# Reordering ScalarE and VectorE work around the norms of a hybrid decoder block: squares, weight splits and form splits put behind other instructions

## The chip, the core and the metric

The kernel runs on one core of one Trainium2 chip. A core has five engines with instruction queues of their own: TensorE (PE: matmuls, with weight loads PEld shown apart), VectorE (DVE), ScalarE (ACT), GpSimd (POOL) and SyncE (SP, which here only issues DMAs). Each queue is worked through in order; engines wait for each other by semaphores. The metric is the device time of one launch in microseconds (us), the median of several runs.

## What is computed

One residual block on 512 tokens of 1024 channels, all float32:

```
z = rms_norm(x) @ w_in                            # pool, rnn, rnn gate and two branch gates
y_pool = pool_mixer(u_pool) @ w_pool_out          # trailing means over 2, 4, 8, 16 tokens
y_rnn  = rg_lru_branch(u_rx, u_rg) @ w_rg_out     # conv, gated linear recurrence, GeLU gate
x2 = x + rms_norm((gate_pool * y_pool + gate_rnn * y_rnn) @ w_o)
up = rms_norm(x2) @ w_up                          # 2 x 3072 columns
hid = gelu(causal_dwconv(up[:, :3072])) * up[:, 3072:]
x3 = x2 + rms_norm(hid @ w_down)
out = x3 + sigmoid(rms_norm(x3) @ w_ple_gate) * rms_norm(p @ w_ple_proj)
```

`rms_norm` divides a token's row by its root mean square and multiplies by a gain. `p` is the per-layer input embedding (256 wide).

## The kernel before

**Three matmuls for one.** TensorE multiplies operands rounded to a shorter form of float32. Each operand is therefore kept as two parts, a *high* part (`hi`, a rounding copy made on ACT) and a *low* part (`lo`, source minus high part, a subtraction on DVE); `split` (line 193) makes both. `mm3` (line 220) issues high x high (line 222), high x low (line 223) and low x high (line 224). So each weight block costs one ACT copy and one DVE subtraction, and a matmul can start when the high parts are there but stops at the second or third step if a low part is late.

**Seven products for eight.** The large products (`w_rg_out`, `w_o`, `w_up`, `w_down`) are cut into two by two blocks and computed with seven block products of sums of blocks. The sums of the activations are called *forms* and numbered 1 to 7: 1, 2 and 4 are blocks themselves, 5, 6, 7 and 3 are differences and sums (`rg_form` for the recurrent branch, `form` and `form_split` for the up product). Sums of weight blocks come partly from DRAM, where DMAs of the POOL queue add them up. The first pair of up blocks (`p == 0`) is computed plainly, with the blocks `PLAIN = (11, 21, 12, 22)` and half the tokens at a time.

**Stages.** TensorE's order is written out by hand. What matters here, with the times of the profile before:
- to 225 us: input product, pool mixer and recurrent branch, ending with the pool branch's output product: eight weights `("wpo", m)`, each of twelve 512-wide matmuls. Beside it the forms of the recurrent branch are made: with weight m goes form `LATE_FORMS[m]`, that is 5, 6, 3, 7, 2 for m = 0 to 4. `weight(key)` prepares four keys ahead (`AHEAD`).
- 225 to 300 us: the seven products with `w_rg_out`, then those with `w_o`.
- 285 to 330 us: the norm and the residual add for four token tiles of 128 tokens. `x2_sum(t)` squares the two halves of a tile on ACT (line 501, sum accumulated and read), adds the sums on DVE (line 512), takes the power -1/2 on POOL (line 496), and multiplies and adds on DVE (lines 999 and 1004). `x2_out(t)` stores the tile, squares it again, and writes the normed tile `h2n` (line 1078). `h2_tile(t)` transposes it on PE (line 1015), splits both halves (line 1034), and copies two blocks of each half in float32 to `h2f` (line 1042), from which the forms are made. The tiles take turns with the embedding's product (`ple_tile(t)`, evacuated by one DVE copy, line 846, and one ACT copy, line 847) and the first up products: blocks 11 and 21, transposes of tile 2, blocks 12 and 22, transposes of tile 3, product (1,1), then the four plain blocks for the other half of the tokens (`O_AFTER`, line 48). `ple_norm(t)` computes the embedding's norms: two squares, sum, power, and a copy to `rp` (line 855).
- 330 to 355 us: first gated tiles. `gated_half` makes the convolution (one ACT and two DVE instructions, lines 1153 and 1155) and the GeLU; the bank is then given back by an ACT copy (line 1201) so that product (1,6) can go on in it. `hidden` (line 1171) multiplies with the other half, after which `up_product` can write its bank (line 1145). Meanwhile the forms 5, 6, 7, 3 are made (line 1207) and split.
- 355 to 545 us: the loop over pairs of up blocks, seven products each; then the down product, the last norms, and the embedding's gate.

**Who sets the order.** On ACT, DVE, POOL and SP a planner orders the instructions: it simulates the program with its own costs and takes, whenever an engine is free, the ready instruction that stands first in the program, where `urgent()` and `high_priority` move instructions forward. `behind(ins, name)` (line 154) is an edge that makes the planner place `ins` after the named instruction of the same engine; it adds no semaphore. `last_copy`, `last_sub` and `last_low` name the newest high copy and low subtraction. A buffer of a pool (`raw`: 6, `t`: 5, `m`: 25, `C` and `A`: 4 each) that is still in use makes its next user wait; two engines never read one PSUM bank at once, the later in the program waits.

**Names in the profile.** `ps` is a PSUM bank, `m` a slot of the `mid` pool, `t` a temporary, `C` and `A` the large tiles that hold activations in two parts, `h` hidden tiles, `raw` a weight as loaded, `s` one column of sums, `rb` the discarded output of a square.

Of the kernel before, what the change touches and what calls it, by code (L numbers as in the profile page):

```python
# [83 lines left out]
def block_kernel(  # L84
# [272 lines left out]

    ready, low_of = {}, {}
    nxt = [0]
# [27 lines left out]
    def up_form(p, f):  # L387
# [21 lines left out]
        else:  # L409
            t = b[p, {2: 21, 3: 22, 5: 0}[f]]  # L410
        if p == 0 and f in PLAIN[2:]:
            late.append((f, t))
            return
        hi, lo = (v.rearrange("p (j c) -> p j c", j=2) for v in parts_of(D))
        split(hi, lo, t)
        if (p, f) == (0, PLAIN[1]):
            behind(last_sub[0], h2n_done[1])
        if p == 1 and f != 1:
# [5 lines left out]
        if p > 1 and f == 3:  # L424
            behind(last_copy[0], z6_done[p])
        ready["up", p, f] = (hi, lo)

    def late_splits():
# [8 lines left out]
    def prep(key):  # L437
# [24 lines left out]
        if key == order[0]:  # L462
            for a, b in FIRST:
                ACT.copy(hi[:, a:b], raw[:, a:b])
                sub(lo[:, a:b], raw[:, a:b], hi[:, a:b].bitcast(F32))
        else:
            ins = ACT.copy(hi, raw)  # L467
            if key[0] == "wpg" and key[2] == 1:
                behind(ins, last_copy[0].ins.name)
            with tc.high_priority(offset=2 * URGENT if key[0] == "wpg" and key[2] == 0 else 300 if key[0] == "in" and key[1] >= 12 else 0):  # L470
                ins = sub(lo, raw, hi.bitcast(F32))
                low_of[key] = ins.ins.name
            if key[0] == "wpg" and key[2] == 1:
                behind(ins, last_low[0])
# [13 lines left out]

    last_pow, last_square = [None], [None]

# [19 lines left out]
    def rstd_from(sums):  # L510
        v = tiny()
        V.scalar_tensor_tensor(v, sums[0], EPS, sums[1], ALU.add, ALU.add)  # L512
        return rsqrt(v)
# [318 lines left out]
    rp = {}  # L832
    h2n_done, h2f_done, z_copied, hid_done, summed = {}, [None], [None], [None], {}
    z6_done, o_done, ple_done, late = {}, {}, {}, []

# [91 lines left out]
    for m in range(KD):  # L927
        w = weight(("wpo", m))
        if m in LATE_FORMS:
            rg_form(LATE_FORMS[m])  # L930
        pas.append(bank())
        for k in range(4):
# [136 lines left out]

    def x2_out(t, after=None):  # L1070
        res = [xr[t, 0], xr[t, 1]]
        for h in range(2):
            nc.sync.dma_start(x2d[t * P : (t + 1) * P, h * S : (h + 1) * S], res[h])
        with urgent():
            r = rstd_of(res, after=after)
            for h in range(2):
                h2n[t, h] = slot()
                ins = V.scalar_tensor_tensor(h2n[t, h], res[h], r, g_pre[h], ALU.mult, ALU.mult)
                h2n_done[t] = ins.ins.name

# [69 lines left out]
    def gated_half(j, pg):  # L1150
        a = temp()
        with urgent():
            ACT.activation(a, pg, AF.Identity, scale=c1(C_FW + 2 * NJ + j), bias=c1(C_FB + j))
            for d in (1, 2):
                V.scalar_tensor_tensor(
                    a[:, d:], pg[:, : S - d], c1(C_FW + (2 - d) * NJ + j), a[:, d:], ALU.mult, ALU.add
                )
        act(a, a, AF.Gelu_apprx_tanh)
        act_g[j] = a
# [14 lines left out]
    for t in range(NT):  # L1174
# [3 lines left out]
        if t == 1:  # L1178
            h2_tile(1)
            late_splits()  # L1180
            x2_out(2, h2_done[0])
            x2_sum(3, (oz[1], o5[:, 1]))
        if t == 2:
            x2_out(3, ple_done[0])
    for t in range(NT):
        ple_norm(t, ple_outs[t], ple_done[0])
    for kind, n in O_AFTER:
        if kind == "tr":
            h2_tile(n)
        elif kind == "up":  # L1190
            up_plain(n, 0)
# [12 lines left out]
    def form(f, a, b, op=ALU.subtract):  # L1204
        for k in (0, 2):
            d[f, k] = slot()
            V.tensor_tensor(d[f, k], a[k], b[k], op)
# [7 lines left out]
    with urgent():  # L1215
        form(5, h2f[21], h2f[22])
        form(6, {k: d[5, k] for k in (0, 2)}, h2f[11])
        form_split(6)
    form_split(5, True)
    form(7, h2f[11], h2f[21])  # L1220
    form_split(7, True)
    form(3, {k: d[6, k] for k in (0, 2)}, h2f[12], ALU.add)
    form_split(3, True)

# [15 lines left out]
    for i in range(2):  # L1240
        hidden(i, ub[i], None)
    down_sums = sums_of("wd")
    for p in range(1, NPAIR + 1):
# [265 lines left out]
```

## Time and profile before

| what | value |
|---|---|
| median of 3 runs | 705.51 us (705.23 to 705.91) |
| profiled execution | 706.08 us, span 704.1 us |
| TensorE busy | 693.9 us, 99% of the span |
| weight loads busy | 638.9 us, 91% |
| VectorE, ScalarE, GpSimd busy | 592.0, 454.1, 95.9 us |
| DMA traffic | 175.71 MB, mean 250 GB/s |
| granted TensorE clock | 1.000 |

The span runs from the first to the last instruction; the launch around it makes up the rest of the profiled execution's time. A row of the timeline has the start and length in us, engine, line of the kernel, operation, output <- inputs by tile name, shapes, and how many like instructions were merged (x2); in brackets stands how long the engine had been idle and what ended that. A CAST is an ACT copy to the short format. L191 is the subtraction of every split, L195 and L467 are its copies, L501 every square of a norm.

### The profile page before, as it was taken

The numbers are of one execution on the slowest core, as the hardware profiler recorded it, in microseconds if no ns is written. First come the engines' busy times: TensorE is split into PE (matmuls) and PEld (weight loads), VectorE is DVE, ScalarE is ACT, GpSimd is POOL, SyncE is SP. The second block draws the span as 40 slices with busy tenths as digits, with TensorE's granted clock in tenths as the row PEclk, the third lists the DMA queues.
The fourth block names the chain that finished last, engine by engine and source line by source line (L and its number), as shares of the span: only waits on it lengthen the run. The fifth ranks groups of instructions, "written<-read, shape, count | busy, mean of one in ns | idle before, by whom it ended". The sixth has DMA issues, their size and how long they took to land.

```text
span 704.1 us, 11599 instructions
## 1 busy us (share of the span) xinstructions
PE 693.9 (99%) x4423; PEld 638.9 (91%) x4423; DVE 592.0 (84%) x772; ACT 454.1 (64%) x693; POOL 95.9 (14%) x123
## 2 busy tenths in 40 slices
PE   9999999999999999998999999999999999999997
PEld 8888888888888998898999999999999888888886
DVE  5698645999749898886999999999999988989972
ACT  5857789934447575478866677666667747666631
POOL 0311231322000000111011211111111210001100
PEclk9999999999999999999999999999999999999999
DMA  8998999999888997864496896897699799968111
GB/s 314 411 305 257 258 244 222 277 259 283 254 316 298 315 366 251 323 216 142 131 322 210 201 249 232 196 249 243 170 223 369 253 300 332 332 213 276 49 61 61
DMA packets 67287, 175.71 MB, mean 250 GB/s; under 512 B 6048, under 2 KB 6688, under 8 KB 66848
## 3 DMA queue, kind: packets, MB, share of 16 engines
q1 hardware_dynamic: 49808, 124.64, 49.4%
q0 software_dynamic: 17280, 50.34, 31.0%
q8 instruction: 35, 0.57, 0.3%
q14 instruction: 20, 0.16, 0.1%
q10 hardware_dynamic: 144, 0.00, 0.0%
HBM read 162.37 MB, written 62.91 MB: 320 GB/s over the span
## 4 chain that ended last, share of the span: by engine, by line
PE 73%; DVE 13%; ACT 6%; DMA 3%; issue 3%; POOL 1%; SPq 0%; DVEq 0%; ACTq 0%
PE ps L222 23%; PE ps L224 23%; PE ps L223 23%; DVE lo L191 3%; PE ps L575 3%; ACT m L166 2%; DVE m L713 1%; DMA parts<-hi 1%; ACT t L166 1%; ACT hi L195 1%; POOL s L496 1%; DVE m L640 1%; DVE t L784 1%; ACT rb L501 1%; PE ps L684 1%
## 5 line engine op out<-in xcount | busy, mean ns | idle before, releaser
L191 DVE TENSOR_TENSOR lo<-raw,hi 128x1024 fp32r<-128x1024 f32 (+2 forms) x199 | 230.4, 1184 | 48.3 <-ACT hi L467 29.3
L222 PE MATMUL ps<-A,hi 128*128 128x256 f32 (+1 forms) x672 | 212.3, 316 | 1.2 <-ACT ps L1145 0.7
L224 PE MATMUL ps<-A,lo 128*128 128x256 f32 (+1 forms) x672 | 211.6, 315 | 0.0
L223 PE MATMUL ps<-A,hi 128*128 128x256 f32 (+1 forms) x672 | 211.6, 315 | 0.0
L467 ACT CAST hi<-raw 128x1024 fp32r<-128x1024 f32 (+1 forms) x118 | 118.2, 1012 | 59.3 <-PE ps L224 19.8
L222 PEld LDWEIGHTS ps<-A,hi 128*128 128x128 f32 x672 | 128.4, 191 | 9.6 <-issue 1.0
L224 PEld LDWEIGHTS ps<-A,lo 128*128 128x128 f32 x672 | 128.4, 191 | 6.8
L223 PEld LDWEIGHTS ps<-A,hi 128*128 128x128 f32 x672 | 128.4, 191 | 6.6
L222 PE MATMUL ps<-C,hi 128*128 128x256 f32 x376 | 103.9, 276 | 1.8 <-ACT C L195 1.1
L223 PE MATMUL ps<-C,hi 128*128 128x256 f32 x376 | 103.4, 275 | 0.3 <-DVE C L191 0.3
L224 PE MATMUL ps<-C,lo 128*128 128x256 f32 x376 | 103.3, 275 | 0.0
L195 ACT CAST hi<-raw 128x1024 fp32r<-128x1024 f32 x78 | 80.6, 1052 | 23.2 <-PE ps L223 13.7
L222 PE MATMUL ps<-hi,A 128*128 128x512 f32 x224 | 85.2, 380 | 0.0
L224 PE MATMUL ps<-hi,A 128*128 128x512 f32 x224 | 85.0, 379 | 0.0
L223 PE MATMUL ps<-lo,A 128*128 128x512 f32 x224 | 85.0, 379 | 0.0
L222 PEld LDWEIGHTS ps<-C,hi 128*128 128x128 f32 x376 | 71.9, 191 | 2.7 <-ACT C L195 1.2
L223 PEld LDWEIGHTS ps<-C,hi 128*128 128x128 f32 x376 | 71.9, 191 | 0.6 <-DVE C L191 0.5
L224 PEld LDWEIGHTS ps<-C,lo 128*128 128x128 f32 x376 | 71.9, 191 | 0.0
L307 POOL DMA_DIRECT2D wdsum<-in_w_down_dram x36 | 33.1, 1056 | 150.0 <-ACT t L1143 63.8
L496 POOL TENSOR_TENSOR s<-s,mhalf 128x1 f32<-128x1 f32 (+1 forms) x21 | 16.1, 769 | 260.6 <-DVE s L512 238.6
L224 PEld LDWEIGHTS ps<-hi,A 128*128 128x128 f32 x224 | 42.4, 189 | 6.0
L223 PEld LDWEIGHTS ps<-lo,A 128*128 128x128 f32 x224 | 42.4, 189 | 5.8
(202 smaller groups left out, 1068.7 us busy)
## 6 DMA issues: line engine op xcount, KB each, us to landing
raw<-in_w_up_dram SPq DMA_DIRECT2D x46, 512.0 KB, 5.7
wdsum<-in_w_down_dram POOLq DMA_DIRECT2D x36, 512.0 KB, 7.6
raw<-in_w_in_dram SPq DMA_DIRECT2D x32, 512.0 KB, 8.8
raw<-wdsum SPq DMA_DIRECT2D x24, 512.0 KB, 8.5
raw<-in_w_down_dram SPq DMA_DIRECT2D x18, 512.0 KB, 7.0
wosum<-in_w_o_dram POOLq DMA_DIRECT2D x12, 512.0 KB, 9.2
wdsum<-wdsum POOLq DMA_DIRECT2D x12, 512.0 KB, 6.3
raw<-wosum SPq DMA_DIRECT2D x8, 512.0 KB, 6.2
```

The lines of the kernel that those rows point to most:

```text
L166: ins = ACT.activation(o, i, func, **kw)
L191: return V.tensor_tensor(o, a, b, ALU.subtract)
L195: last_copy[0] = ACT.copy(hi, src)
L222: PE.matmul(o, ah, bh, start=start, stop=False, **kw)
L223: PE.matmul(o, ah, bl, start=False, stop=False, **kw)
L224: PE.matmul(o, al, bh, start=False, stop=stop, **kw)
L307: ins = nc.gpsimd.dma_start(o, i, **kw)
L467: ins = ACT.copy(hi, raw)
L496: last_pow[0] = nc.gpsimd.tensor_tensor(y, v, mhalf[:, :n], ALU.pow).ins.name
L501: ins = ACT.activation(rb, v, AF.Square, scale=1.0 / 32.0, accum_out=s)
L575: PE.matmul(rx[m], a[:, o : o + P], turns(b), start=k == 0 and i == 0, stop=k == KD - 1 and i == 2)
L640: return V.tensor_tensor(row(o), back(ps), row(rb), ALU.mult)
```

## The change

No instruction is added or removed; the order on ACT and DVE and the place in the program change, in five parts:
1. *Branch forms behind pool weights.* The copy and subtraction of the branch form made with weight m are put behind those of weight m + 4 (at most 7).
2. *Three up weights late.* Of the plain blocks, 21 now joins 12 and 22 in `late`: split in `late_splits`, its copy behind token tile 1's last copy (line 1042), its subtraction behind that of tile 1. Before, its split came with its load, the subtraction behind normed tile 1.
3. *Fourth norm's sum first.* `x2_sum(3)` comes ahead of `x2_out(2)` in the program, and normed tile 2 goes behind the fourth tile's sum of squares.
4. *Embedding squares behind token tiles' copies.* `ple_norm` of embedding tiles 0 and 1 goes behind tile 2's copies, of 2 and 3 behind tile 3's copies; before, all four stood behind the last embedding tile's copy.
5. *Third up form behind gated tiles.* The subtractions of weights (1,5) and (1,7) leave the place beside their copies: that of (1,5) goes behind the convolution of the second gated tile, that of (1,7) behind `hidden`. Form 3's split goes behind `hidden` too, and its two float32 blocks are taken from the pool `t` instead of `m`.

```diff
-        if p == 0 and f in PLAIN[2:]:
+        if p == 0 and f != PLAIN[0]:
             late.append((f, t))
             return
         hi, lo = (v.rearrange("p (j c) -> p j c", j=2) for v in parts_of(D))
+        if (p, f) in ((1, 5), (1, 7)):
+            ins = ACT.copy(hi, t)
+            behind(ins, h2_done[0])
+            later[f] = hi, lo, t
+            ready["up", p, f] = (hi, lo)
+            return
         split(hi, lo, t)
-        if (p, f) == (0, PLAIN[1]):
-            behind(last_sub[0], h2n_done[1])
...
+    def later_low(f):
+        hi, lo, t = later[f]
+        last_sub[0] = sub(lo, t, hi.bitcast(F32))
+        last_low[0] = last_sub[0].ins.name
...
             ins = ACT.copy(hi, raw)
+            last = ins.ins.name
...
                 low_of[key] = ins.ins.name
+                copy_of[key] = last
...
     def rstd_from(sums):
         v = tiny()
-        V.scalar_tensor_tensor(v, sums[0], EPS, sums[1], ALU.add, ALU.add)
+        last_stat[0] = V.scalar_tensor_tensor(v, sums[0], EPS, sums[1], ALU.add, ALU.add).ins.name
         return rsqrt(v)
...
         if m in LATE_FORMS:
             rg_form(LATE_FORMS[m])
+            behind(last_copy[0], copy_of["wpo", min(m + AHEAD, KD - 1)])
+            behind(last_sub[0], low_of["wpo", min(m + AHEAD, KD - 1)])
...
-    def x2_out(t, after=None):
+    def x2_out(t, after=None, stat=None):
...
                 ins = V.scalar_tensor_tensor(h2n[t, h], res[h], r, g_pre[h], ALU.mult, ALU.mult)
-                h2n_done[t] = ins.ins.name
+                if stat is not None:
+                    behind(ins, stat)
...
             for d in (1, 2):
-                V.scalar_tensor_tensor(
+                ins = V.scalar_tensor_tensor(
                     a[:, d:], pg[:, : S - d], c1(C_FW + (2 - d) * NJ + j), a[:, d:], ALU.mult, ALU.add
                 )
+        conv_done[0] = ins.ins.name
...
             h2_tile(1)
             late_splits()
-            x2_out(2, h2_done[0])
             x2_sum(3, (oz[1], o5[:, 1]))
+            x2_out(2, h2_done[0], last_stat[0])
         if t == 2:
             x2_out(3, ple_done[0])
-    for t in range(NT):
-        ple_norm(t, ple_outs[t], ple_done[0])
     for kind, n in O_AFTER:
         if kind == "tr":
             h2_tile(n)
+            for t in (n - 2) * 2, (n - 2) * 2 + 1:
+                ple_norm(t, ple_outs[t], h2f_done[0])
...
-            d[f, k] = slot()
+            d[f, k] = temp() if f == 3 else slot()
...
     form_split(5, True)
+    later_low(5)
+    behind(last_sub[0], conv_done[0])
     form(7, h2f[11], h2f[21])
     form_split(7, True)
     form(3, {k: d[6, k] for k in (0, 2)}, h2f[12], ALU.add)
-    form_split(3, True)
...
     for i in range(2):
         hidden(i, ub[i], None)
+    later_low(7)
+    behind(last_sub[0], hid_done[0])
+    form_split(3, True)
+    behind(last_sub[0], hid_done[0])
```

More of the change, by code (lines that the diff above doesn't have):

```diff
@@ L356, in block_kernel @@
             plan(("wpg", kp, h), rows2(w_ple_gate, kp, h))
-    ready, low_of = {}, {}
+    ready, low_of, copy_of = {}, {}, {}
     nxt = [0]
@@ L487, in pick @@
         return t[0][:, a:b], t[1][:, a:b]
-    last_pow, last_square = [None], [None]
+    last_pow, last_square, last_stat = [None], [None], [None]
     rb = const.tile([P, S], F32, tag="rb", name="rb")
@@ L832, in block_kernel @@
     rp = {}
-    h2n_done, h2f_done, z_copied, hid_done, summed = {}, [None], [None], [None], {}
-    z6_done, o_done, ple_done, late = {}, {}, {}, []
+    h2f_done, z_copied, hid_done, summed = [None], [None], [None], {}
+    z6_done, o_done, ple_done, late, later, conv_done = {}, {}, {}, [], {}, [None]
     def ple_tile(t):
```

## The prediction

> **What bounds the kernel now.** I read the page first, then busy time by stretches of 10 us, then the waits of TensorE, then the timeline at each place where TensorE stood still. A difference under 0.2%, some 1.4 us, is about what a measurement of this kernel can't tell from none.
>
> ```profile
> span 704.1 us, 11599 instructions
> PE 693.9 (99%) x4423; PEld 638.9 (91%) x4423; DVE 592.0 (84%) x772; ACT 454.1 (64%) x693; POOL 95.9 (14%) x123
> ```
>
> TensorE (PE) is the bound: its order is fixed by hand, and a time saved counts only if PE had been waiting. The stretches, columns PE, weight load (PEld), DVE, ACT and POOL busy, clock, DMA share and GB/s, show where it did:
>
> ```profile
> 200.00:210.00 10.00, 10.00 (x48) 8.79 (x47) 3.88 (x5) 4.61 (x7) 0.00 (x0) 1.00 0.84 329
> 210.00:220.00 10.00, 9.36 (x44) 7.90 (x43) 9.74 (x13) 7.33 (x10) 0.00 (x0) 1.00 0.98 344
> 320.00:330.00 10.00, 7.89 (x64) 7.08 (x63) 5.25 (x14) 7.48 (x24) 2.08 (x4) 1.00 0.41 151
> 340.00:350.00 10.00, 8.77 (x76) 8.39 (x75) 9.39 (x15) 9.85 (x17) 0.00 (x0) 1.00 0.30 95
> 390.00:400.00 10.00, 10.00 (x92) 10.00 (x91) 10.00 (x13) 8.05 (x13) 3.12 (x3) 1.00 0.70 177
> 400.00:410.00 10.00, 10.00 (x92) 10.00 (x91) 8.84 (x9) 5.65 (x11) 1.03 (x1) 1.00 1.10 223
> ```
>
> Between the first load and the tail PE idles in three stretches alone: 0.64, 2.11 and 1.23 us. The clock is 1.00 throughout, so no time hides there. The waits of PE name them (us in all, times, longest); the sum of these six rows, 4.0, is the idle of the three stretches:
>
> ```profile
> PE ps L222 <- ACT C L195: 1.1, 1, 1.1
> PE ps L222 <- ACT ps L1145: 0.7, 1, 0.7
> PE ps L222 <- ACT m L1042: 0.7, 2, 0.6
> PE ps L224 <- DVE lo L191: 0.6, 1, 0.6
> PE ps L222 <- ACT ps L1201: 0.5, 1, 0.5
> PE ps L223 <- DVE C L191: 0.3, 1, 0.3
> ```
>
> Idle understates what a wait costs, because matmuls overlap. Two waits by the starts:
>
> ```profile
> 213.36 0.38 PE L223 MATMUL ps<-m,hi 128*128 128x512 f32 x1
> 214.38 0.48 PE L224 MATMUL ps<-m,lo 128*128 128x512 f32 x1 [0.64 <-DVE lo L191]
> 214.70 0.38 PE L222 MATMUL ps<-m,hi 128*128 128x512 f32 x1
> ...
> 348.24 0.28 PE L224 MATMUL ps<-A,lo 128*128 128x256 f32 x1
> 349.26 0.38 PE L222 MATMUL ps<-A,hi 128*128 128x256 f32 x1 [0.75 <-ACT ps L1145]
> ```
>
> Undisturbed, 512-wide matmuls start 0.21 apart (48 in the 10 us from 200) and 256-wide ones 0.11 (92 in the 10 us from 390). The first wait makes steps of 1.02 and 0.32 out of two of 0.21: it costs 0.92, the last 0.11 of it in a slow first step. The second makes 1.02 out of 0.11, 0.91, and 1.02 with such a step behind it. So a wait costs its idle time plus about 0.27. Seven waits (the third row has two) of 3.98 us idle cost 3.98 + 7 x 0.27 = 5.9 us: 0.9 at the first place (A), 2.11 + 4 x 0.27 = 3.2 at the second (B), 1.23 + 2 x 0.27 = 1.8 at the third (C). That is all that can be had.
>
> By the idle time of matmuls alone it would be 3.98. The Trainium skill (Perfetto Trace Analysis, Identifying the Most-Contended Engine) calls matmul busy time a poor measure, since pipelined instructions look smaller, and would have the weight loads' busy time read instead; by that, each stretch against a full one of its kind, (8.79 - 7.90) + (10.00 - 7.08) + (10.00 - 8.39) = 5.4 us are open. The steps between starts side with the page.
>
> **Place A, branch forms behind pool weights.** Queues of ACT and DVE at the wait:
>
> ```profile
> 209.69 2.00 ACT L195 CAST A<-C 128x1024 fp32r<-128x1024 f32 x2
> 211.59 0.61 ACT L467 CAST hi<-raw 128x512 fp32r<-128x512 f32 x1
> 213.63 0.62 ACT L467 CAST hi<-raw 128x512 fp32r<-128x512 f32 x1 [1.43 <-DMA raw<-in_w_pool_out_dram]
> ...
> 210.76 2.36 DVE L191 TENSOR_TENSOR A<-C,A 128x1024 fp32r<-128x1024 f32 x2 [0.26 <-ACT A L195]
> 213.64 1.33 DVE L191 TENSOR_TENSOR lo<-raw,hi 128x512 fp32r<-128x512 f32 x2
> ```
>
> PE waits for the low part of the fifth pool-out weight, which runs at 213.64 behind the low parts of branch forms 5 and 6 (2.36), as its high part ran behind their copies (2.00). The change adds no instruction; it puts each form behind the weight four ahead. Without the forms in front the copy can run near 209.7 and the low part end by 211; PE wants it at 213.58. Next late is the sixth weight: its load ends at 213.6, its two parts by about 215.0, and PE wants the low part at 213.58 + 12 x 0.215 = 216.2, so 1.1 us are left. The forms are first used when this product ends, ten us on; they wait in the same queues, and the loads behind them stay in their order on SP. Gain 0.9; bounds 0 and 0.9, and I take the whole, the cover being 1.1.
>
> **Place B, the last token tiles.** These rows hold the chain:
>
> ```profile
> 313.06 0.61 ACT L847 COPY m<-ps 128x512 f32<-128x512 f32 x1
> 313.85 1.46 POOL L496 TENSOR_TENSOR s<-s,mhalf 128x1 f32<-128x1 f32 x1 [2.80 <-DVE s L512]
> 319.17 0.54 POOL L496 TENSOR_TENSOR s<-s,mhalf 128x1 f32<-128x1 f32 x1 [3.87 <-DVE s L512]
> 319.75 1.41 DVE L1078 SCALAR_TENSOR_TENSOR m<-m,s,m 128x512 f32<-128x512 f32 x2 [0.66 <-POOL s L496]
> 321.68 1.28 DVE L191 TENSOR_TENSOR C<-ps,C 128x512 fp32r<-128x512 f32 x2
> 322.12 1.04 PE L1015 MATMUL ps<-ident,m 128*128 128x128 f32 x8
> 322.40 0.37 ACT L1042 COPY m<-ps 128x256 f32<-128x256 f32 x1 [2.67 <-DVE C L191]
> 327.51 1.05 ACT L195 CAST C<-ps 128x512 fp32r<-128x512 f32 x2
> ```
>
> and, as one row for the squares (L501) in a stretch, with ACT's busy time:
>
> ```profile
> 318.90:329.30 10.40, 5.84 (x16) 1.00 0.51 168
> ```
>
> PE stands at 323 and 325 for the copies of token tile 2 (L1042), and at 327 and 328 for the high and low parts of tile 3, whose transposes ended at 323.15 (322.12 + 1.04). Tile 2's copies waited for its low parts (321.68), those for the normed tile 3 (319.75), that for the fourth norm's sum, whose power ran only at 313.85. Between the copies, and ahead of tile 3's casts, stand the eight squares of the embedding's norms with their accumulator reads, 5.84 in all, 0.73 each.
>
> Fourth sum first: its inputs come out of the product that ends ahead of the embedding tiles, so its two squares (1.5), sum, power and two adds can follow the third sum's at once, some ten us earlier, on POOL too ahead of the third tile's power. The normed tile 3 then hangs on the copy of embedding tile 2 (L847, 313.06) alone: 313.7, two squares 1.5, power 0.54, 1.41, and the 0.7 of hand-overs give 317.9 instead of 321.2. Low parts of tile 2 then end at 319.2, its copies by 320, when PE wants them at 323.0: both L1042 waits go, with 3 us to spare. The other side: tile 1's casts are pushed back by up to 1.5 on ACT, against the 1.1 that the third edit frees in front of its low parts.
>
> Squares behind the copies: four (2.9 us) now run between tile 2's copies and tile 3's casts, 320 to 323, four behind tile 3's copies. Tile 3's casts start at about 323.2, low parts end by 325.6; PE wants them from 323.0 + 24 x 0.11 = 325.6 on, half 0 first, whose low part ends at 324.9. Both waits go. The embedding tiles hold their slots no longer than 3 us more, while slots come free from the residual tiles.
>
> Up weights late: the copy and low part (1.2) of block 21 move from in front of tile 1's low parts to behind tile 1's copies, ahead of 12 and 22. Tile 1's low parts so start 1.1 earlier. I put tile 1's copies at 310, the high part of 21 at 311, its low part at 312.1 to 313.3 (the latter if DVE first runs the normed tile 2, 1.4). PE reaches block 21 72 matmuls of 0.11 and eight transposes (0.9) ahead of 322.12, at 313.2, and wants its low part at 313.4. This is the tightest spot. Its raw buffer is freed 4 us later, so the load of block (1,5), then pled and x2d stores behind it on SP, start later; their users come 20 us on.
>
> Bounds for B: 3.2, and 3.2 less a stall at block 21 of up to 1.4 + 0.92 + 0.27 = 2.6. The 0.92 is the power's 1.46 against 0.54: it is slow here when a low part runs beside it. On this the Trainium skill (GPSIMD Engine Reference, Specifications) says that POOL shares its SBUF interfaces with VectorE and contends with VectorE instructions of two SBUF inputs, which a low part has; by it three late low parts near these powers speak against the change, and the rival below takes it up. I take 2.8: full gain less one scrap of 0.4, the size of the smallest wait there is (the third row of PE's waits has 0.7 in two, the longest 0.6, which leaves some 0.15 idle, plus 0.27), nearer to the estimate of the copies than to the far bound.
>
> **Place C, into the first transformed products.** First the low parts (L191) among the conv's steps as one row with DVE's busy time, then the two queues:
>
> ```profile
> 336.20:340.40 4.20, 2.42 (x2) 1.00 0.72 219
> ```
>
> ```profile
> 340.31 0.74 DVE L1155 SCALAR_TENSOR_TENSOR t<-ps,col,t 128x510 f32<-128x510 f32 x1
> 347.07 0.69 DVE L191 TENSOR_TENSOR A<-m,A 128x512 fp32r<-128x512 f32 x1 [0.61 <-ACT A L195]
> 347.68 1.28 DVE L1171 TENSOR_TENSOR h<-t,ps 128x512 f32<-128x512 f32 x2
> 348.88 6.90 DVE L191 TENSOR_TENSOR lo<-raw,hi 128x1024 fp32r<-128x1024 f32 x6
> ...
> 338.69 0.36 ACT L1201 COPY ps<-ps 128x256 f32<-128x256 f32 x1 [2.11 <-DVE t L1155]
> 348.84 0.63 ACT L1145 ACTIVATE ps<-ps 128x256 f32<-128x256 f32 x2
> ```
>
> The first wait is for L1201, which needs the last conv step (340.31), behind two low parts, (1,5) and (1,7), 2.42 together. Moved behind the conv, they bring it 2.4 forward; the wait was 0.5. The second is for L1145, which needs the gated tiles (347.68), behind form 3's low parts (2 x 0.6) and 0.61 of waiting for their copy. With form 3 and the low part of (1,7) behind, 1.2 + 1.2 + 0.6 = 3.0 fall out ahead of L1171. But PE arrives 2.8 earlier by place B. DVE starts this stretch with tile 3's low parts, which also end earlier, 325.6 against 329.4, or 3.8; two of the four embedding norms, each with a wait of DVE for POOL of 0.66 as at 319.75, add 1.3. So the gated tiles end near 349.0 - 3.8 - 3.0 + 1.3 = 343.5 and the (1,7) product is due at 349.26 - 1.8 - 2.8 = 344.7 (place A shifts all alike). L1145 needs 0.4 of that; the moved low part of (1,7) runs until 344.7 and is wanted at 344.9. Form 3's temporaries take the last two of the five temp buffers, which are free then; its product comes 8 us later. The cost lies between 0 and today's wait with its restart, 1.0 once more; one scrap, 0.4, is near the middle. C gains 1.8 - 0.4 = 1.4.
>
> **Sum.** 0.9 + 2.8 + 1.4 = 5.1 us. The profiled execution took 706.08 (its span and 1.98 around it), so 701.0 by its own time; it lies 0.57 above the median of 705.51, and the median so comes to 700.4. The loop behind keeps PE full with DVE at 8.84 and 10.00 of 10, so it passes the gain on, and the tail is untouched.
>
> **Rivals.**
> 1. *Block 21 is late* (or tile 1's copies ahead of it). For: three us of room shrink to 0.1 to 1.3; a slow power adds 0.92. Against: ACT and DVE lose 1.5 us of squares and a low part in front. PE waits up to 2.6 and the gain is 5.9 - 2.6 - 0.4 = 2.9: 702.6.
> 2. *ACT and DVE stay the bound at C.* The chain of waits runs through ACT, DVE and POOL from 300 to 349; ACT is at 9.85 of 10 there. If the four squares (2.9) land ahead of the conv and forms, C's waits come back, doubled: 5.9 - 3.6 = 2.3: 703.2. Against it: ACT idled 2.11 ahead of L1201.
> 3. *The moves do nothing*: the planner had ordered so by its own costs and shifts its fillers into the new holes; each wait is replaced by one like it: 705.5. Against it: each new order is an edge that it has to keep.
> 4. *Slower.* The loop's order shifts: 3.6 us of low parts (1,7), form 3, (1,4) are pushed to where six already stand in a row (348.88, 6.90), and the six raw buffers turn later. If in each of the ten turns PE then waits for one low part behind an add, 1.2 us, the whole is 12 - 5.9 = 6.1 slower: 711.6. It decides from (5.9 + 1.4)/10 = 0.73 a turn. Against it: the loop's code is the same, it shows no idle PE, and a delay that comes once is paid once.
>
> **How the numbers follow.** Forecast with scraps from none to twice those taken, 699.6 to 701.2: 0.58. Rival 1: 0.14. Rival 2: 0.13. Rival 3: 0.05. Rival 4: 0.10. The range from 699.5 (nothing waits, less the spread of the runs) to 704.0 holds the first three, 0.85. Faster 0.85, same 0.05, slower 0.10.
>
> **What would show it.** Right: PE's waits for L1145, L1201, L1042 and tile 3's parts are gone from its list; the stretch 210 to 220 has PE at 10.00; L501 squares of the sum stand before tile 1's casts; L1155 follow each other on DVE without a low part of 1.21 between. Wrong: a new wait of PE for DVE lo L191 near 313, or for L1145 again, or idle PE spread over 350 to 540.

## The result

| what | before | after |
|---|---|---|
| median of 6 runs each | 705.52 us (705.23 to 706.27) | 703.09 us (702.49 to 703.40) |
| profiled execution | 706.08 us, span 704.1 us | 702.84 us, span 701.1 us |

The ratio of after to before is 0.9963, 95% interval 0.9950 to 0.9976. The change gains 2.4 us by the medians and 3.0 by the spans, of 5.9 that were open. Forecast was 700.4 us, from 699.5 to 704.0, with 0.85 for faster: the sign and the range hold, and the time is 2.7 above the likeliest. It also lies above 701.2, the end of what the forecast itself allowed; the range holds it because it took in the first two rivals.

**The profile after.** In the changed kernel's lines L512 is the square (L501 before), L523 the sum (L512), L507 the power (L496), L1017 the residual add (L1004), L1091 the normed tile (L1078), L857 and L858 the embedding's copies (L846, L847), L1055 the tile's copies (L1042), L1169 the conv steps (L1155), L1216 the bank's copy (L1201), L1159 the bank that waits for the gated tiles (L1145). The first lines of the page:

```profile
span 701.1 us, 11599 instructions
PE 693.4 (99%) x4423; PEld 638.2 (91%) x4423; DVE 591.6 (84%) x772; ACT 454.2 (65%) x693; POOL 97.5 (14%) x123
```

TensorE's busy time fell by 0.5 us only; its standing still fell from 10.2 us (704.1 - 693.9) to 7.7. Its waits (us in all, times, longest), where the second and fourth row belong to the first microseconds:

```profile
PE ps L224 <- DVE lo L191: 1.3, 1, 1.3
PE ps L241 <- DVE mhalf L235: 1.1, 1, 1.1
PE ps L222 <- ACT ps L1216: 0.5, 1, 0.5
PE ps L586 <- ACT hi L473: 0.2, 1, 0.2
```

The rows for L1145, L1042 and tile 3's high parts have gone, and so has the old wait for DVE lo L191, at 214 us. That for L1216 is the old L1201, at its old size. The row at the top is new: it is block 21, the first rival. Busy time by stretches (PE, PEld, DVE, ACT, POOL, clock, DMA share, GB/s):

```profile
310.00:320.00 10.00, 8.69 (x78) 8.50 (x77) 8.69 (x13) 7.62 (x15) 1.08 (x2) 1.00 0.70 229
320.00:330.00 10.00, 10.00 (x90) 9.86 (x89) 5.99 (x13) 9.23 (x25) 1.09 (x2) 1.00 0.41 131
330.00:340.00 10.00, 9.47 (x85) 9.28 (x85) 9.41 (x17) 9.17 (x16) 3.52 (x2) 1.00 0.25 90
```

The old place B (320 to 330) is full; the idle time now stands at 312 and at 338. Both by the starts of matmuls:

```profile
312.31 0.28 PE L223 MATMUL ps<-C,hi 128*128 128x256 f32 x1
313.89 0.38 PE L224 MATMUL ps<-C,lo 128*128 128x256 f32 x1 [1.31 <-DVE lo L191]
314.11 0.28 PE L222 MATMUL ps<-C,hi 128*128 128x256 f32 x1
...
338.41 0.28 PE L224 MATMUL ps<-A,lo 128*128 128x256 f32 x1
339.21 0.38 PE L222 MATMUL ps<-A,hi 128*128 128x256 f32 x1 [0.53 <-ACT ps L1216]
339.43 0.28 PE L223 MATMUL ps<-A,hi 128*128 128x256 f32 x1
```

Against 0.11 a step, the first costs 1.58 + 0.22 - 2 x 0.11 = 1.57 us, the second 0.80 + 0.22 - 0.22 = 0.80. Three scraps that the profile of before lacks cost 0.23 (271.5), 0.22 (326.2) and 0.33 (348.6). So 5.9 - 1.57 - 0.80 - 0.78 = 2.75 are gained, and some 0.3 come from the wait for the first load, which was 0.3 shorter in this execution: 3.0, the difference of the spans.

**A measure for the place.** Two landmarks of TensorE's fixed order cut the span in three: the first product step behind the transposes of token tile 0, and the one behind those of the first tile of the last norms. In the changed kernel:

```profile
295.62 0.46 PE L222 MATMUL ps<-hi,A 128*128 128x512 f32 x1
...
644.26 0.46 PE L222 MATMUL ps<-hi,A 128*128 128x512 f32 x1
```

| kernel | to the first | between | from the second to the end |
|---|---|---|---|
| before | 296.62 | 350.65 | 56.8 |
| after | 295.62 | 348.64 | 56.8 |
| part 1 alone | 295.18 | 350.78 | 56.8 |
| low part of 21 ahead of normed tile 2 | 296.00 | 349.42 | 56.8 |
| block 21 early (part 2 undone) | 296.58 | 347.97 | 56.8 |
| sums of forms behind the conv | 295.84 | 348.44 | 56.8 |
| part 4 undone | 295.22 | 349.10 | 56.8 |
| part 3 undone | 296.49 | 348.85 | 56.8 |
| part 5 undone | 295.53 | 349.14 | 56.8 |
| embedding's norms at the end | 295.55 | 347.37 | 58.5 |
| the same, block 21 early | 295.12 | 345.72 | 58.6 |
| the same, low part of 21 ahead | 295.52 | 346.29 | 58.5 |
| block 21 early, two norms behind the last | 297.62 | 345.72 | 58.0 |

Places B and C and the loop lie between. There the change gains 2.0 us, of 5.0 open; place A and the first load give 1.0. In the first column all kernels with part 1 (all but before) run the same work up to the first landmark, and differ by 2.5 us from one execution to the next. So spans and single times mislead by as much as the steps in question, and the experiments on B and C are read by the middle column. Each row is one execution. Two pairs show how well the column repeats: before and part 1 alone, with the same work in between, differ by 0.13, and the two kernels at 345.72 are alike up to the last few us. A difference of 0.2 is hardly more than that.

**Why block 21 is late.** VectorE's queue ahead of it, with ScalarE's cast:

```profile
307.36 0.75 DVE L1017 SCALAR_TENSOR_TENSOR m<-t,s,m 128x512 f32<-128x512 f32 x1 [0.66 <-POOL s L507]
308.03 1.28 DVE L191 TENSOR_TENSOR C<-ps,C 128x512 fp32r<-128x512 f32 x2
...
310.70 1.42 DVE L1091 SCALAR_TENSOR_TENSOR m<-m,s,m 128x512 f32<-128x512 f32 x2 [0.65 <-POOL s L507]
312.03 0.68 DVE L857 COPY m<-ps 128x512 f32<-128x512 f32 x1
312.63 3.48 DVE L191 TENSOR_TENSOR lo<-raw,hi 128x1024 fp32r<-128x1024 f32 x3
...
308.75 0.38 ACT L1055 COPY m<-ps 128x256 f32<-128x256 f32 x1 [2.90 <-DVE C L191]
310.42 2.02 ACT L195 CAST hi<-raw 128x1024 fp32r<-128x1024 f32 x2
```

The high part of 21 was there at 311.4, but VectorE was inside normed tile 2 until 312.1 and then took the embedding's copy. Its low part is the first of the three at 312.63 and ended at 313.84; TensorE had wanted it at 312.42.

**Why L1216 is late.** VectorE among the conv steps:

```profile
334.07 0.74 DVE L1169 SCALAR_TENSOR_TENSOR t<-ps,col,t 128x511 f32<-128x511 f32 x1
...
334.80 0.68 DVE L1222 TENSOR_TENSOR m<-m,m 128x512 f32<-128x512 f32 x1
335.40 0.74 DVE L1169 SCALAR_TENSOR_TENSOR t<-ps,col,t 128x510 f32<-128x510 f32 x1
...
336.12 0.68 DVE L1222 TENSOR_TENSOR t<-m,m 128x512 f32<-128x512 f32 x1
...
337.98 0.74 DVE L1169 SCALAR_TENSOR_TENSOR t<-ps,col,t 128x510 f32<-128x510 f32 x1
```

No low part of 1.21 stands between them, as announced. In their place stand four float32 sums of forms 7 and 3 (L1222, 0.60 to the next start; two are shown), 2.4 us, as much as the two low parts that left.

### The profile page after: what moved, and what is told of

Read it like the earlier page. It is cut to its first block, busy times and chain, and to the rows that moved or that the text cites. A ratio compares the mean times of both kernels' runs of the same rounds, so it can differ in the third digit from the quotient of the medians.

```text
span 701.1 us, 11599 instructions
## 1 busy us (share of the span) xinstructions
PE 693.4 (99%) x4423; PEld 638.2 (91%) x4423; DVE 591.6 (84%) x772; ACT 454.2 (65%) x693; POOL 97.5 (14%) x123
## 4 chain that ended last, share of the span: by engine, by line
PE 89%; DVE 5%; ACT 1%; issue 1%; POOL 1%; DMA 1%; SPq 0%; ACTq 0%; DVEq 0%; POOLq 0%
PE ps L222 28%; PE ps L224 28%; PE ps L223 28%; PE ps L586 3%; POOL s L507 1%; DVE lo L191 1%; PE ps L695 1%; DMA raw<-in_w_rx_dram 1%; DVE C L191 1%; DVE m L1017 1%; PE ps L1028 0%; DMA x2d<-m 0%; DVE m L1091 0%; DVE m L1222 0%; ACT rb L512 0%
## 5 line engine op out<-in xcount | busy, mean ns | idle before, releaser
L191 DVE TENSOR_TENSOR lo<-raw,hi 128x1024 fp32r<-128x1024 f32 (+2 forms) x199 | 230.3, 1183 | 47.0 <-ACT hi L476 30.3
L195 ACT CAST hi<-raw 128x1024 fp32r<-128x1024 f32 x76 | 78.6, 1051 | 20.2 <-PE ps L223 13.1
L507 POOL TENSOR_TENSOR s<-s,mhalf 128x1 f32<-128x1 f32 (+1 forms) x21 | 17.6, 840 | 265.6 <-DVE s L523 243.8
L224 PEld LDWEIGHTS ps<-hi,A 128*128 128x128 f32 x224 | 42.3, 189 | 6.3 <-DVE A L191 0.4
L222 PEld LDWEIGHTS ps<-hi,A 128*128 128x128 f32 x224 | 42.3, 189 | 6.0
```

What stands on the lines that cost most here:

```text
L191: return V.tensor_tensor(o, a, b, ALU.subtract)
L195: last_copy[0] = ACT.copy(hi, src)
L222: PE.matmul(o, ah, bh, start=start, stop=False, **kw)
L224: PE.matmul(o, al, bh, start=False, stop=stop, **kw)
L507: last_pow[0] = nc.gpsimd.tensor_tensor(y, v, mhalf[:, :n], ALU.pow).ins.name
```

## The experiments

Two theories stood against each other. One: each part of the change takes away its own wait, so what is left is block 21 (part 2's fault) and the four sums. The other: from 300 to 350 us the lists of ScalarE and VectorE themselves are the bound, and a reorder only chooses where TensorE waits. In each kernel but the first the edit is made to the changed kernel; line numbers move by a few with each edit. The kernels ran on several chips, so each ratio is against the kernel before on the same chip. Apart from part 1 alone, all their intervals overlap that of the change, 0.9950 to 0.9976, so what is said of single edits rests on the waits and the landmarks.

### Part 1 alone

The kernel before, with the branch forms behind the pool weights and nothing else.

```diff
+            copy_of[key] = ins.ins.name
...
             rg_form(LATE_FORMS[m])
+            behind(last_copy[0], copy_of["wpo", min(m + AHEAD, KD - 1)])
+            behind(last_sub[0], low_of["wpo", min(m + AHEAD, KD - 1)])
```

> The kernel before with part 1 alone (branch forms behind pool weights). Theory: the wait of 0.64 at the fifth pool-out weight goes and nothing else moves, so 0.9 us less than before, about 704.6, with TensorE's other six waits (1.1, 0.7, 0.7 in two, 0.5, 0.3) as they were. Rival: the forms, now later, or the shifted weights cost as much further on, so no difference to before and a new wait near 216 or in the recurrent product from 223.

705.36 us against 705.85 on the same chip, ratio 0.9990 (0.9979 to 1.0002), span 702.8. Place A's wait is gone from TensorE's list, nothing came in its stead, and the six later waits stand there with their old sizes (1.1, 0.8 in two, 0.8, 0.5, 0.3). The waits show the 0.9; the medians, 0.5 apart, neither show it nor exclude it, and the first column (1.4 less) scatters by more. VectorE's queue came forward with TensorE: token tile 1's low parts start at 307.09 here and at 308.53 before, 1.44 earlier, like the landmark.

### Low part of block 21 ahead of normed tile 2

```diff
             behind(last_sub[0], low)
+            low_21.append(last_sub[0].ins.name)
...
                     behind(ins, stat)
+                    behind(ins, low_21[0])
```

> The changed kernel with one more edge: the two normed halves of tile 2 go behind the low part of block 21 on VectorE. In the changed kernel TensorE waits 1.31 us at 312.6 for that low part, which runs at 312.63 behind the normed tile 2 (310.70, 1.42) and an embedding copy (0.68), while its high part is done at 311.4. Theory (VectorE's order is the cause): the low part starts at 311.4 and ends at 312.5, so 0.1 to 0.3 of the wait stays, and the kernel gets 1.2 to 1.5 us faster than the changed one, about 701.7. Rival (ScalarE is the cause, the high part comes too late): the wait keeps 1 us or more and the time stays near 703. Second rival: the normed tile 2, 1.1 later, makes its transposes at 316 wait, and the gain is lost there.

704.21 us, ratio 0.9982 (0.9966 to 0.9998): slower by the medians than the change as it is. The waits of TensorE:

```profile
PE ps L223 <- DVE C L191: 0.8, 1, 0.8
PE ps L222 <- ACT C L195: 0.6, 1, 0.6
PE ps L222 <- ACT ps L1218: 0.5, 1, 0.5
PE ps L224 <- DVE lo L191: 0.3, 1, 0.3
```

Block 21 fell from 1.31 to 0.33, but tile 3's parts wait again, 0.63 and 0.75. VectorE stood idle for the high part ahead of the low one, and everything behind it moved back:

```profile
312.02 1.23 DVE L191 TENSOR_TENSOR lo<-raw,hi 128x1024 fp32r<-128x1024 f32 x1 [1.49 <-ACT hi L195]
...
321.01 1.28 DVE L191 TENSOR_TENSOR C<-ps,C 128x512 fp32r<-128x512 f32 x2
```

Tile 2's low parts run at 321.01 in place of 319.90 (0.4 of this is the later start of this execution), its copies, the squares and tile 3's casts follow, while TensorE, held 1.0 less at block 21, comes for them earlier. In the middle column this costs 0.8: the cheap mending gives more back than it saves.

### Block 21 split early, as before

```diff
-        if p == 0 and f != PLAIN[0]:
+        if p == 0 and f in PLAIN[2:]:
...
+        if (p, f) == (0, PLAIN[1]):
+            behind(last_sub[0], h2n_done[1])
```

> The changed kernel with part 2 undone for block 21: it is split with its load again, its low part behind normed tile 1. Theory (part 2 made the new wait, and the rest of place B pays by itself): the wait at 312.6 goes, the wait of 1.57 us in all with it, and the time is near 701.6. Rival (part 2 was needed: the low part of 21, 1.1 us on VectorE in front of tile 1's low parts, which already came at 308.0 in the changed kernel, pushes them past the first up product): a wait of 0.5 to 1 us at the start of block 11, at 309.5, and a time of 702 to 703.

702.71 us, ratio 0.9961 (0.9947 to 0.9975), span 701.3. Part 2 undone, the 1.57 us of block 21 vanish, and 0.7 are gained between the landmarks: part 2 is a loss there as it stands. By the ratios, 0.9961 and 0.9963, the two kernels are alike. The rest went to tile 3's low part, which now waits 0.75, by starts 1.1, and the bank's copy waits 0.5 as ever:

```profile
PE ps L223 <- DVE C L191: 0.8, 1, 0.8
PE ps L222 <- ACT ps L1220: 0.5, 1, 0.5
```

### Sums of forms 7 and 3 behind the conv

```diff
-            V.tensor_tensor(d[f, k], a[k], b[k], op)
+            ins = V.tensor_tensor(d[f, k], a[k], b[k], op)
+            if f in (7, 3):
+                behind(ins, conv_done[0])
```

> The changed kernel with the four sums of forms 7 and 3 behind the last convolution step on VectorE. In the changed kernel the wait for the copy that gives the bank back stayed (0.53 idle, 0.8 us by the starts) though the two low parts are gone from between the convolution steps: four sums of 0.6 stand there now. Theory (they are the cause): the last step comes 1.2 or more earlier, the wait goes, 0.8 us less than the changed kernel, about 702.3. Rival (ScalarE is the cause: the second convolution's first instruction comes only at 334.9, behind squares and casts): the last step stays within 0.5 us of 338.0 and the wait keeps more than half of its length.

702.87 us, ratio 0.9961 (0.9942 to 0.9979), span 701.1; 0.2 less between the landmarks. The wait for L1216 went, so with the four sums elsewhere the copy is in time (it is too with part 4 undone, below: more than one thing in the queues stood in its way); but ten us later another bank is late:

```profile
PE ps L224 <- DVE lo L191: 1.6, 2, 1.3
PE ps L222 <- ACT ps L1161: 0.6, 1, 0.6
```

```profile
349.15 1.04 ACT L195 CAST hi<-raw 128x1024 fp32r<-128x1024 f32 x1 [0.71 <-DMA raw<-up2sum]
350.10 0.37 ACT L1161 COPY ps<-ps 128x256 f32<-128x256 f32 x1
```

TensorE comes 0.8 earlier to a copy that stands behind a cast whose weight has not landed.

### Parts 4, 3 and 5, each undone

Part 4 undone (the embedding's squares where they were), then part 3, then part 5:

```diff
+    for t in range(NT):
+        ple_norm(t, ple_outs[t], ple_done[0])
     for kind, n in O_AFTER:
         if kind == "tr":
             h2_tile(n)
-            for t in (n - 2) * 2, (n - 2) * 2 + 1:
-                ple_norm(t, ple_outs[t], h2f_done[0])
```

> The changed kernel with part 4 undone: the embedding's eight squares behind the last embedding copy again. Theory (part 4 pays most at place B): squares stand between tile 2's copies and ahead of tile 3's casts again, TensorE waits for L1055 and for tile 3's parts 1 to 2.5 us in all (before: 2.11), the wait of 1.31 at block 21 stays and hides part of it; 1 us or more slower than the changed kernel, 704 or above. Rival (part 4 is worth nothing, since the wait at block 21 gives ScalarE the time for the squares): same waits as the changed kernel, 703.

702.84 us, ratio 0.9956 (0.9940 to 0.9972), span 701.1: part 4 is worth nothing here. Tile 3's low part waits 0.4 (0.7 by starts), the bank's copy, 0.8 by starts with part 4, no longer waits. Of the 349.10 between the landmarks 0.68 lie in a wait at 604 us, far from the edit, which no other kernel shows; without it the stretch takes 0.2 less than with part 4.

```diff
+            x2_out(2, h2_done[0])
             x2_sum(3, (oz[1], o5[:, 1]))
-            x2_out(2, h2_done[0], last_stat[0])
```

> The changed kernel with part 3 undone: tile 2's own squares ahead of the fourth norm's sum. Theory (part 3 pushes tile 1's low parts back: one add of 0.75 and 0.66 of waiting for the power stand in front of them, so they start at 308.0): they start about 1 us earlier, the wait at block 21 shrinks from 1.31 to 0.5 or less, but normed tile 3 is late again, 319 or later, and waits for tile 2's copies or tile 3's parts of 1 us or more come back; 703 to 704. Rival (part 3 is free for block 21): its wait stays at 1.2 or more and the waits for tiles 2 and 3 come on top, 705.

703.89 us, ratio 0.9977 (0.9967 to 0.9987), span 702.1. Block 21 has no wait, and tile 3's parts wait 0.6 and 0.8. Tile 1's low parts on VectorE, here and in the kernel before:

```profile
306.86 1.28 DVE L191 TENSOR_TENSOR C<-ps,C 128x512 fp32r<-128x512 f32 x2
...
308.53 1.28 DVE L191 TENSOR_TENSOR C<-ps,C 128x512 fp32r<-128x512 f32 x2
```

Counted from each kernel's own first landmark that is 10.4 us here and 11.9 before, where block 21's low part still stood in front; in the changed kernel (308.03) it is 12.4. So the fourth norm's two steps and its hand-over from POOL pushed them back by 2.0. Part 3 thus both takes away the waits at tile 3 and, together with part 2, makes the one at block 21. Between the landmarks it is worth 0.2; the rest of the 1.0 by the spans lies ahead of the first landmark, where the work is the same, so how much of the 0.8 by the medians is the edit's stays open.

```diff
-        if (p, f) in ((1, 5), (1, 7)):
-            ins = ACT.copy(hi, t)
...
-    later_low(5)
-    behind(last_sub[0], conv_done[0])
...
+    form_split(3, True)
...
-    later_low(7)
-    behind(last_sub[0], hid_done[0])
-    form_split(3, True)
-    behind(last_sub[0], hid_done[0])
```

> The changed kernel with part 5 undone: low parts of (1,5) and (1,7) beside their copies, form 3 ahead of the gated tiles. Theory (part 5 took the wait for L1145 away, 0.75 idle and 1.0 by the starts, and left that for the bank copy as it was): a wait for L1159, which is that line here, of 0.7 or more comes back, the one for L1216 stays near 0.5 or grows by the two low parts; 704.1. Rival (the wait went because TensorE came later, from block 21): no wait for L1159 and 703.

703.65 us, ratio 0.9967 (0.9954 to 0.9981), span 701.5. The wait for the bank's copy grew to 0.9, the one for L1145 stayed away. Part 5 is worth 0.5 between the landmarks, mostly at the first of C's waits. The second, 1.0 of the sum, goes without it, but by little: its bank was given back at 346.40 and TensorE came for it at 346.47, after waits at block 21 and at the bank's copy. With part 5 the bank was free 1.0 ahead (344.98 against 346.01). Whether the wait returns without part 5 once those two are gone wasn't run.

### The embedding's squares taken out of the stretch

The second theory says that less work between 300 and 350 us, not another order, ends the waits. The embedding's four tiles are loaded back for the last stage anyway; here their norms are taken there, which takes eight squares (5.84 us of ScalarE) and four hand-overs from POOL to VectorE out of the stretch. The result is the same norm of the same values.

```diff
-            for t in (n - 2) * 2, (n - 2) * 2 + 1:
-                ple_norm(t, ple_outs[t], h2f_done[0])
...
+            for t in range(NT):
+                ple_norm(t, [ple[t // 2][:, 2 * (t % 2) + h, :] for h in range(2)], None)
```

> The changed kernel, but the embedding's norms are taken at the end, from the embedding tiles that are loaded back there in any case: eight squares (5.84 us of ScalarE), four sums and four powers leave the stretch 320 to 336. Theory (ScalarE and VectorE are the bound from 300 to 350, and part 4 only carries the squares from one full stretch into the next): the wait for the bank copy L1216 (0.53) goes with them, tile 3's parts come 1 us earlier, and only the wait of 1.31 at block 21 is left; 702.0. Rival (the order of VectorE's sums and low parts is the bound, not the load): the wait for L1216 stays at 0.4 or more and the time at 703. Second rival: the squares make the last norms late, with new waits of TensorE between 640 and 670.

703.99 us, ratio 0.9975 (0.9961 to 0.9990), span 701.4; 1.3 less between the landmarks, 1.7 more behind them. From 320 us to the second landmark TensorE is full; block 21 stays, as its cause stands ahead of the squares; and a new wait comes at the end:

```profile
PE ps L224 <- DVE lo L191: 1.4, 1, 1.4
PE ps L1028 <- DVE h L1351: 1.3, 1, 1.3
```

Then with block 21 split early as well (the edit shown above):

> The kernel with block 21 split early again and the embedding's norms at the end as well. With block 21 early alone, its wait went and one of 0.75 for tile 3's low parts came, behind two waits of VectorE for the embedding's sums and powers. Theory (the load is the bound): both go, no wait of TensorE over 0.3 is left from 200 to 640, and all but 0.3 or so of the 5.9 us of the forecast is had: 700.2 us, 2.9 below the changed kernel. Rival (there is always another instruction in the way): a wait of 0.5 or more in 300 to 355, 701.5 or above.

701.77 us (701.17 to 702.25), ratio 0.9942 (0.9930 to 0.9955), span 699.4: the lowest median of all. Between the landmarks 4.9 of the 5.0 open at B and C are gained. The stretches show TensorE full:

```profile
310.00:320.00 10.00, 10.00 (x92) 10.00 (x92) 9.36 (x13) 6.40 (x14) 1.57 (x2) 1.00 0.80 271
...
330.00:340.00 10.00, 10.00 (x92) 10.00 (x91) 9.60 (x15) 9.21 (x15) 0.00 (x0) 1.00 0.23 82
```

Block 21 is early here and tile 3 is not late, the very pair that excluded each other above. That is the second theory's case. Load and order aren't fully parted by it: the edit takes out ScalarE's squares and also VectorE's waits for four sums and powers, and in the changed kernel VectorE was busy only 5.99 of the 10 us from 320 (ScalarE 9.23). And with the low part of 21 ahead of normed tile 2 in its stead:

> The changed kernel with the low part of block 21 ahead of normed tile 2 and the embedding's norms at the end. With the first edit alone 0.33 of the wait at block 21 was left and waits of 0.63 and 0.75 for tile 3's parts came back. Theory (load): these two go with the squares, 0.33 at block 21 stays (0.6 by the starts), 700.7. Rival: normed tile 2 and 3, now 1.1 later on VectorE, keep tile 2's copies and tile 3's parts late by themselves; a wait of 0.5 or more there, 701.7 or above.

702.12 us (702.02 to 702.21), ratio 0.9948 (0.9934 to 0.9962), span 700.3, with 0.3 at block 21 and the same 1.3 at the end. That wait costs 1.6 us by starts. In the 701.77 kernel ScalarE runs ahead of it the last of the embedding's squares (rb<-A), and only then the first of the last two norms (rb<-ps):

```profile
650.13 0.63 ACT L514 ACTIVATE rb<-A 128x512 f32<-128x512 f32 x1
650.95 0.60 ACT L514 ACTIVATE rb<-ps 128x512 f32<-128x512 f32 x1
```

### The late squares behind the last norms

The 701.77 kernel, with the norms of embedding tiles 2 and 3 behind the last norms' squares:

```diff
-            for t in range(NT):
+            for t in (0, 1):
...
             x3_add(3)
+            for t in (2, 3):
+                ple_norm(t, [ple[1][:, 2 * (t % 2) + h, :] for h in range(2)], last_square[0])
```

> The changed kernel with block 21 split early and the embedding's norms taken at the end, as in the best kernel so far, but the four squares of tokens 2 and 3 stand behind the squares of the last two x3 norms instead of ahead of them. The theory that ScalarE's in-order list is what made the new wait at 657 us: the square of the bank of x3's third norm starts at about 648.5 instead of 650.95, the 1.3 us wait of the transposes of tile 3's normed x3 is under 0.3, no wait of TensorE between 200 us and the end of the last product is above 0.4, and the time is 701.77 - 1.5 = 700.3 us (699.8 to 700.9). The rival, that this wait is the chain of the last two norms itself (square, sum, power, add, product by the gains) whatever stands ahead of it: the wait stays at 1.0 or more and the time is 701.5 to 701.9. A second rival, that the squares behind the norms now hold the scale of tokens 2 and 3, and so the first multiplications of the last tiles: a wait of TensorE for a bank or for VectorE of 0.5 or more after 660 us, time above 701.0.

702.52 us (700.76 to 704.15), ratio 0.9952 (0.9937 to 0.9967): no better, and of a wide spread. The tail is 0.6 shorter, not 1.5. The profiled execution, 703.26 with a span of 701.3, has three waits behind the first microseconds:

```profile
PE ps L224 <- DVE lo L191: 0.9, 1, 0.9
PE ps L224 <- DVE h L191: 0.8, 1, 0.8
PE ps L224 <- DVE A L191: 0.6, 1, 0.6
```

The wait at 657 is gone, so the squares in front had made it. The second row, at 665, has the second rival's sign but not its mechanism: token tile 2's low parts stand on VectorE behind a scale that waits for POOL and two output steps, 1.1 us by starts, and that scale is the one of the norm of x3 itself; those of embedding tiles 2 and 3 come only from 667 on. The other two rows stand at 224 and 273 us, where this kernel's instructions and their order are those of the 701.77 kernel; in this execution VectorE was already late at 190:

```profile
190.97 1.22 DVE L191 TENSOR_TENSOR lo<-raw,hi 128x1024 fp32r<-128x1024 f32 x1 [4.89 <-ACT hi L478]
```

In the other twelve executions the same subtraction starts between 188.45 (the 701.77 kernel) and 191.06 (block 21 split early), after a high part that itself came late. What delays it wasn't tried. Against the 701.77 kernel POOL's DMA queue took more of the engines' time from 170 to 215 us, 25.5% for 19.0%; but it was 23.7% in the kernels before and after, which had no wait at 224.

## Why the prediction was right or wrong

**Place A, right.** The whole 0.9 came, and part 1 alone shows it without the rest. The room behind it is smaller than the cover of 1.1 that was counted for the sixth weight: the low part of the next product's first weight ended 2.1 us before TensorE wanted it in the kernel before (222.52, 224.63) and 0.2 before in the changed one (223.18, 223.40). In two executions of kernels with part 1 TensorE waited for it, 0.24 (sums behind the conv) and 0.85 (the last kernel): the place that the first experiment's rival had named. One execution of the kernel before can't say whether it ever waits there too.

**Place B, half right.** The waits at 322 to 329 left, 3.2 us; two of them, 0.6 and 0.8 idle, come back when the fourth sum's step is undone. The step that failed is "the tightest spot": the low part of block 21 was to be there at 312.1, or at 313.3 behind normed tile 2, and to be wanted at 313.4. Counted from the first landmark, which the changed kernel reaches 1.0 earlier, that is 15.5 or 16.7, and 16.8; measured were 18.2 (313.84) and 16.8 (312.42). So the demand was right, and the low part came 1.5 later than even the later of the two. The forecast let tile 1's low parts start 1.1 earlier and charged part 3 to ScalarE alone, with up to 1.5. ScalarE's casts of tile 1 came no later (8.5 behind the landmark in both kernels, 305.15 and 304.15); on VectorE the fourth norm's two steps and its hand-over put the low parts 2.0 back, and that was counted as nothing. Behind them the sum had normed tile 2, but neither its hand-over from POOL (0.65) nor the embedding's copy (L857, 0.60 to the next start). In place of one scrap of 0.4, block 21 cost 1.57. That is the first rival's mechanism at 1.57 of its 2.6; its power of 1.46 had no part in it, the powers at 306.78 and 310.12 took 0.54.

**The squares, wrong.** "Both waits go" was put down to the squares behind the copies among others; with them undone the time is the same (702.84 against 703.09). In their new place, ahead of tile 3's casts and beside the conv steps, they cost again what they freed: 0.7 less at tile 3, 0.8 more at the bank's copy.

**Place C, half right.** The step "moved behind the conv, they bring it 2.4 forward" failed: the low parts left, and the planner took the next ready work, four sums of 0.6. The wait for L1201 stayed at 0.80 by starts, as the second and third rival have it. The second wait went, 1.0. The prediction credited part 5 and place B together; undoing part 5 does not bring it back, by 0.07 us, so the other parts were just enough there and part 5 is what gives room (1.0).

**The sum.** 0.9 + 2.8 + 1.4 was taken. By the same places it is 0.9, 3.2 - 1.57 - 0.22 = 1.4, and 1.8 - 0.80 - 0.33 = 0.7, less 0.2 at 271 us: 2.8. The landmarks agree: B and C brought 2.0 for 4.2. What failed as a whole is that the moves at B and C were costed one by one. At these two places the runs show one queue of work: as the tables above have it, taking one wait away brought another up further on, which took back half of it or more, until work left the stretch. That 703.09 lies in the range is owed to the width that the rivals gave it: it is nearly rival 2's time, 703.2, by losses at block 21 and at C that no rival had together.

**The loop and rival 4.** The loop passed the gain on, as forecast: behind 353 us TensorE has no step longer than in the same place before.

## What to carry to other kernels

Where the helper engines are the bound of a stretch, a reorder that frees one instruction is worth only what the in-order queue doesn't fill again: ask what is ready next, not only what stands in front. Cost a moved step on every queue that it touches: the fourth sum was priced on ScalarE and not on VectorE, where it weighed 2.0. Count all times of such a stretch from one TensorE step, since the helpers' queues come forward with it. When each single fix moves the wait, take work out of the stretch: moving the embedding's norms to the end, with block 21 early, brought 3.8 us by medians on one chip (705.61 to 701.77) where the reorder alone brought 2.4; the two ratios, 0.9942 and 0.9963, have intervals that overlap, so the step from one to the other is likely, not settled.

## What the runs showed of the hardware

**A power of one column beside back-to-back subtractions.** In the changed kernel, POOL's power twice, and what VectorE ran beside the second:

```profile
323.51 0.54 POOL L507 TENSOR_TENSOR s<-s,mhalf 128x1 f32<-128x1 f32 x1 [6.71 <-DVE s L523]
330.77 2.60 POOL L507 TENSOR_TENSOR s<-s,mhalf 128x1 f32<-128x1 f32 x1 [5.14 <-DVE s L523]
...
330.54 1.22 DVE L191 TENSOR_TENSOR lo<-raw,hi 128x1024 fp32r<-128x1024 f32 x1
331.68 1.28 DVE L191 TENSOR_TENSOR A<-m,A 128x512 fp32r<-128x512 f32 x2
```

The second began in one subtraction and ended at 333.37, 0.4 after the last of three in a row; the prediction had 1.46 for the worst. The Trainium skill (GPSIMD Engine Reference, Specifications) says that POOL's interfaces are shared and contend with VectorE instructions of two SBUF inputs; these rows agree. VectorE waited 0.44 for this one, an embedding norm.

**Idle time understates a wait.** Block 21's wait shows 1.31 us of idle time and costs 1.57 by starts; the 256-wide step behind a wait took 0.22 in place of 0.11 each time.
